# A depth-wise convolution of 31 taps: six tiles on TensorE with two positions per product, a shifted tile read by two transfers

## The chip, the cores and the metric

One core of a Trainium2 chip runs the whole program. The time is the device time of one execution in microseconds (us). Five engines each work through their own list of instructions: TensorE (PE), VectorE (DVE), ScalarE (ACT), GpSimd (POOL) and SyncE (SP). SP computes nothing and issues most of the transfers; POOL and ACT can issue transfers too. The transfers are carried by 16 DMA engines.

## What is computed

The program is one step of a network of four layers over 384 positions (128 of a prompt, 256 of a sample, each a sequence of its own) and 1024 channels. Each layer is a mixer and an MLP. The mixer of layer 1, the only one of its kind, is a convolution block:

```python
def _dwconv_centred(x, w, b):
    k = w.shape[0]
    lo = (k - 1) // 2
    hi = k - 1 - lo
    y = lax.conv_general_dilated(x, w[:, None, :], window_strides=(1,), padding=[(lo, hi)],
                                 dimension_numbers=('NWC', 'WIO', 'NWC'),
                                 feature_group_count=x.shape[-1])
    return y + b

def _conformer_conv(h, w_pw1, b_pw1, dw_w, dw_b, ln_g, ln_b, w_pw2, b_pw2):
    val, gate = jnp.split(h @ w_pw1 + b_pw1, 2, axis=-1)
    z = val * jax.nn.sigmoid(gate)
    z = _dwconv_centred(z, dw_w, dw_b)
    z = jax.nn.silu(_layernorm(z, ln_g, ln_b))
    return z @ w_pw2 + b_pw2
```

Here `w_pw1` is 1024 x 2048 and `dw_w` holds 31 taps for each of the 1024 channels. Everything is fp32.

## The kernel before

Channels lie on partitions, so a tensor of 1024 channels is eight tiles of 128 partitions by 384 positions. A dense fp32 product is split in high and low parts and done as three products (`mm3`). Weights come in chunks of 1 MB (`raw`, two buffers) and are split on ACT (`whi`) and DVE (`wlo`). PE runs through products of this kind while the transfers, ACT and DVE prepare the next chunk. Each engine takes its instructions in the order in which the build has put them: that of the code, moved in places by `issue_after`, which keeps what is written under it behind a named instruction.

The function `conformer` does the mixer of layer 1. For each tile m, `pwin(m)` runs the pw1 chunk on PE, and `glu` makes the gated tile on ACT (`gth`, `gv`) and DVE and writes it into `zp`, with zeros between and beside the two sequences. The convolution is then done in one of two ways. Tiles 0 and 1 are done on DVE, a multiply and add over 399 positions for each tap (`conv_dve`, L903). Tiles 2 to 7 are done on PE: `glu` writes `zp` to DRAM (`zd`, L854) and reads it back by four transfers, each into 32 partitions and shifted by one position more than the last (`z`, L857). A partition of `z` then holds four channels at one of four shifts, and one product with diagonals of taps (`dg`, L861, read from `diag`) sums four taps of 32 channels. A tile takes 8 steps of 4 groups of 32 channels: 32 products of 399 columns (`conv_mm`). The sums (`cps`, in PSUM) go directly to `zc`, on ACT for the tiles in FIRST (L885), else on DVE (L887). The buffer `z4` exists three times. The transfers for tiles 2 to 5 are issued by POOL, those for tiles 6 and 7 by SP.

The layer norm sums over channels, so over all eight tiles. A provisional mean from four tiles (FIRST; `shift`, products `mu1p`) is taken off first; `moments` then adds each tile into one sum (`me1a`) and its square into another (`va1a`). Tile 7 comes last and in two pieces (`stats`): the sample's 256 columns, then the prompt's 128. PE sums over channels by products with ones (`lnm` for the mean, `lnv` for the variance), and a short chain on ACT and DVE makes the factor of the norm. `normed` scales each tile, applies silu, and splits it (`yh`, `yl`) for the pw2 product (`p`). Weights of the modulation that are needed here (`pmwl`) are loaded by `lnload`, the last two into buffers of `z4`. `preload` brings an activation table to ACT ahead of its use.

Of the kernel before, what the change touches and what calls it, by code (L numbers as in the profile page):

```python
# [28 lines left out]
CG = SEQ + 15 + LAT  # L29
CSEG = ((0, 0, SEQ), (1, SEQ + 15, CG))  # L30
CP = CG + CW
PE_CONV = (2, 3, 4, 5, 6, 7)
TAP = CW // 4 + 1
SYNCZ = (6, 7)
CONVCUT = 20
ZW = CG + 4 * (TAP - 1)

# [55 lines left out]
FIRST = (2, 3, 0, 4)  # L93
# [26 lines left out]
def trunk(ctx, tc, wst, wmod, vecs, condr, xin, kcT, vcache, rpbt, diag, ident_in,  # L120
# [81 lines left out]
    loaded = {}  # L202

    def load_chunk(i):
# [616 lines left out]
    def conformer(l, j, nrm):  # L821
        mv = need(l, G1)
        with (tc.tile_pool(name=f"cf{l}", bufs=1) as cp,
              tc.tile_pool(name=f"cd{l}", bufs=1, space=bass.MemoryType.DRAM) as dp):
            zps = [cp.tile([P, CP], F32, tag="zp", name=f"zp{l}{i}", bufs=KT) for i in range(KT)]
# [4 lines left out]
            def glu(m, pv, pg, c=None):  # L830
# [14 lines left out]
                for s, a, b in SEG:  # L845
                    o = 15 + 15 * s
                    i = nc.vector.scalar_tensor_tensor(z[:, a + o:b + o], th[:, a:b], 1.0, v[:, a:b],
                                                       op0=ALU.add, op1=ALU.mult)
                glus.append(i.ins)
                if m in PE_CONV:  # L850
                    z4 = cp.tile([P, 4, ZW], F32, tag="z4", name=f"z4{l}{m}", bufs=3)
                    zd = dp.tile([P, CP], F32, tag="zd", name=f"zd{l}{m}", bufs=3)
                    dma = (nc.sync if m in SYNCZ else nc.gpsimd).dma_start
                    dma(zd, z)  # L854
                    zg = zd.rearrange("(g c) n -> c g n", g=4)
                    for s in range(4):
                        i = dma(z4[32 * s:32 * s + 32], zg[:, :, s:s + ZW])  # L857
# [21 lines left out]
            def conv_pe(m):  # L879
                zcs[m] = zc = cp.tile([P, N], F32, name=f"zc{l}{m}")  # L880
                ps = conv_mm(m, f"cps{l}{m}", 0, CG)
                for s, a, e in CSEG:
                    _, xa, xb = SEG[s]
                    if m in first:
                        nc.scalar.activation(zc[:, xa:xb], ps[:, a:e], AF.Identity, bias=dwb[:, m:m + 1])  # L885
                    else:
                        nc.vector.scalar_tensor_tensor(zc[:, xa:xb], ps[:, a:e], dwb[:, m:m + 1], mu[:, xa:xb],  # L887
# [502 lines left out]
```

## Time and profile before

| | us |
|---|---|
| median of 3 runs | 1750.3 (1749.62 to 1750.89) |
| profiled execution | 1750.85 |
| its span | 1748.7 |
| second pw1 piece of the chain to the last variance sum of the sample, within the span | 461.17 to 559.45 |

The granted TensorE clock over the span was 0.997 of full speed. The part that the change touches is some 100 us of 1749. In the profile a line like `x cps L131` names the engine's operation by the tile that it writes; L131 is the helper through which all products go, so products are told apart by tile names. For a transfer the profile gives the time of its issue on the queue of an engine (SPq is that of SP) and, apart from that, the time from issue to landing. Of the convolution's reads back from DRAM POOL issues 16 and SP 8, of 213.5 KB each.

### The profile page before, as it was taken

To read this page: it belongs to the slowest core of one execution; us is meant where nothing else is said; L and a number is where in the kernel's file an instruction comes from. 1 tells how busy PE (TensorE), PEld (TensorE's weight loads), DVE (VectorE), ACT (ScalarE), POOL (GpSimd) and SP (SyncE) were. 2 spreads that over 40 slices of the span, in tenths; PEclk is the share of its full clock that TensorE was granted. 3 is DMA by queue.
4 is the path that set the end of the run, shared out by engine and by line. 5 is a ranking of instruction groups with operands and counts; after the bars stand their busy time and mean duration, and the time that the engine had idled before them with its cause. 6 is when DMAs were issued, how large, how long until landed. Compare 5 with 4: busy or idle time off the path is not lost.

```text
span 1748.7 us, 27296 instructions
## 1 busy us (share of the span) xinstructions
PE 1723.2 (99%) x10442; PEld 1625.2 (93%) x10442; DVE 1404.8 (80%) x2791; ACT 945.0 (54%) x1697; POOL 16.1 (1%) x36
## 2 busy tenths in 40 slices
PE   8999999999999999999999999999999999999997
PEld 7779999999986999999987889999999789999997
DVE  5998999899897898889875668889999978843443
ACT  4876672454633774254465657524546976733531
POOL 0000000000020000000000000000000000000000
PEclk9999999999999999999999999999999999999999
DMA  9665367766486247767554433676774413533331
GB/s 389 236 219 177 128 225 254 239 246 236 159 237 180 97 139 259 240 219 241 195 182 140 133 99 130 205 240 235 242 241 162 155 49 121 174 128 121 124 135 43
DMA packets 67795, 322.42 MB, mean 184 GB/s; under 512 B 7952, under 2 KB 13456, under 8 KB 44496
## 3 DMA queue, kind: packets, MB, share of 16 engines
q1 hardware_dynamic: 66384, 316.30, 52.8%
q0 software_dynamic: 1280, 4.38, 1.0%
q8 instruction: 82, 1.34, 0.3%
q14 instruction: 49, 0.40, 0.1%
HBM read 316.69 MB, written 3.96 MB: 183 GB/s over the span
## 4 chain that ended last, share of the span: by engine, by line
PE 77%; DVE 15%; ACT 3%; issue 2%; DMA 2%; SPq 0%; DVEq 0%; ACTq 0%
PE f L131 29%; PE o L131 27%; PE pw L131 4%; PE lo L131 3%; DVE mjunk L331 3%; PE qk L131 3%; DVE wlo L219 2%; PE p L131 2%; PE wo L131 2%; PE cps L131 2%; PE v L131 2%; DVE xf L608 1%; DMA pmw<-wmod 1%; PE s L131 1%; PE po L131 1%
## 5 line engine op out<-in xcount | busy, mean ns | idle before, releaser
L218 ACT ACTIVATE whi<-raw 128x1024 fp32r<-128x1024 f32 x360 | 378.5, 1059 | 545.3 <-PE o L131 327.2
L219 DVE TENSOR_TENSOR wlo<-raw,whi 128x1024 fp32r<-128x1024 f32 x360 | 437.7, 1221 | 165.6 <-ACT whi L218 165.3
L331 DVE SCALAR_TENSOR_TENSOR mjunk<-dmw,condb 128x1024 bf16<-128x1024 f32 x308 | 375.3, 1219 | 1.5
L131 PE MATMUL o<-hl,whi 128*128 128x384 f32 x1024 | 343.0, 335 | 0.0
L131 PE MATMUL o<-hh,wlo 128*128 128x384 f32 x1024 | 343.0, 335 | 0.0
L131 PE MATMUL o<-hh,whi 128*128 128x384 f32 x1024 | 343.0, 335 | 0.0
L131 PEld LDWEIGHTS o<-hh,wlo 128*128 128x128 f32 x1024 | 192.2, 188 | 0.0
L131 PEld LDWEIGHTS o<-hh,whi 128*128 128x128 f32 x1024 | 192.2, 188 | 0.0
L131 PEld LDWEIGHTS o<-hl,whi 128*128 128x128 f32 x1024 | 192.2, 188 | 0.0
L501 DVE SCALAR_TENSOR_TENSOR x<-o,modv,x 128x128 f32<-128x128 f32 (+1 forms) x128 | 47.4, 412 | 69.0 <-PE o L131 69.0
L131 PE MATMUL g<-xf,graw 128*128 128x386 f32 x256 | 85.7, 490 | 1.7 <-DVE gl L666 1.7
L131 PEld LDWEIGHTS g<-xf,graw 128*128 128x128 f32 x256 | 47.9, 190 | 34.3 <-DVE gl L666 2.3
L785 DVE TENSOR_TENSOR hl<-s,hh 128x384 fp32r<-128x384 f32 x128 | 71.1, 555 | 6.6 <-ACT s L784 2.4
L783 ACT ACTIVATE hh<-r 128x384 fp32r<-128x384 f32 x128 | 67.1, 524 | 3.3
L784 ACT ACTIVATE s<-r 128x384 f32<-128x384 f32 x128 | 65.2, 509 | 0.0
L779 ACT ACTIVATE r<-f 128x384 f32<-128x384 f32 x112 | 53.0, 473 | 13.4 <-PE f L131 13.4
L131 PE MATMUL lo<-yh,wlo 128*128 128x384 f32 x128 | 43.5, 340 | 1.6 <-DVE wlo L219 1.6
L131 PE MATMUL lo<-yl,whi 128*128 128x384 f32 x128 | 43.0, 336 | 0.0
L131 PE MATMUL lo<-yh,whi 128*128 128x384 f32 x128 | 42.6, 336 | 0.0
L903 DVE SCALAR_TENSOR_TENSOR zt<-zp,vec,zt 128x399 f32<-128x399 f32 x58 | 36.7, 633 | 1.4
L131 PE MATMUL wo<-oT,whi 128*128 128x384 f32 x128 | 33.7, 343 | 0.0
L131 PE MATMUL cps<-z,dg 128*32 128x399 f32 (+2 forms) x448 | 32.8, 449 | 0.0
(1515 smaller groups left out, 4002.2 us busy)
## 6 DMA issues: line engine op xcount, KB each, us to landing
raw<-wst SPq DMA_DIRECT2D x180, 1024.0 KB, 5.0
dmw<-wmod SPq DMA_DIRECT2D x154, 512.0 KB, 4.1
pmw<-wmod SPq DMA_DIRECT2D x34, 512.0 KB, 6.8
graw<-wst SPq DMA_DIRECT2D x16, 512.0 KB, 4.8
bt<-rpbt SPq DMA_DIRECT2D x16, 384.0 KB, 3.5
z<-zd POOLq DMA_DIRECT2D x16, 213.5 KB, 6.7
dg<-diag SPq DMA_DIRECT2D x6, 512.0 KB, 4.1
pmwl<-wmod SPq DMA_DIRECT2D x4, 512.0 KB, 5.0
```

Of the source, the lines that this page charges most:

```text
L131: i = nc.tensor.matmul(*a, **kw)
L218: nc.scalar.activation(hi, raw[:, s], AF.Copy)
L219: nc.vector.tensor_tensor(lo, raw[:, s], hi.bitcast(F32), op=ALU.subtract)
L331: nc.vector.scalar_tensor_tensor(mjunk, w, 0.5, condb[:, s], op0=ALU.mult, op1=ALU.mult, accum_out=mod_tile(l)[:, c, m, s:s + 1]))
L501: nc.vector.scalar_tensor_tensor(x[m][:, xa:xb], ps[:, a:b], mv[:, g, m, s:s + 1], x[m][:, xa:xb], op0=ALU.mult, op1=ALU.add)
L608: nc.vector.scalar_tensor_tensor(xf, r[:, k:k + LG], lcw[:, j, t, k:k + 1], xf, op0=ALU.mult, op1=ALU.add)
L779: nc.scalar.activation(r, ps[:, :N], AF.Relu)
L783: nc.scalar.activation(hh, r, AF.Square)
L784: nc.scalar.activation(s, r, AF.Square)
L785: nc.vector.tensor_tensor(hl, s, hh.bitcast(F32), op=ALU.subtract)
L903: nc.vector.scalar_tensor_tensor(t, z[:, k:k + CG], dww[:, m, k:k + 1], t, op0=ALU.mult, op1=ALU.add)
```

## The change

Tiles 1 to 6 are done on PE with two positions in one product; tile 7 stays with one position per product, and only tile 0 is left on DVE. For tiles 1 to 6 `glu` writes the even and the odd positions of `zp` apart, and the copy in DRAM is kept so. The shifted tile is read by two transfers of 64 partitions, one for each parity. Each has four shifts outermost, then 16 rows of channels, then one run of 1717 numbers that spans eight channels' rows. A partition thus holds eight channels at one of eight shifts. A product has 32 output rows, 16 channels by two neighbouring positions, and 200 columns: 2 halves of the channels, 4 steps, 4 groups, so 32 products of 200 columns for a tile (`conv_pair`). The rows of its result alternate between the two positions. ACT copies it from PSUM (`co`), and four transfers on ACT's queue bring it to `zq`, where a partition holds one channel. `conv_in` adds the bias and takes off the mean, on ACT for tiles 1 to 3, on DVE for tiles 4 to 6.

Tile 7's shifted tile is read by one transfer to 128 partitions, with four shifts outermost, 32 rows, and a run of 1724. The channels of tiles 1 to 7 then have another order on the partitions behind the convolution; the rows of pw2, the bias and the factors of the norm are put in that order on the host. The provisional mean comes from tiles 0 to 3, and its products move ahead of the end of the last pw1 chunk. The transfers of tile 5 move from POOL's queue to SP's. The third `pmwl` gets a buffer of its own and the other three use those of `z4`. `preload` moves ahead of the copy of tile 6, and the first part of pw2 is kept behind the norm's instructions of tile 5. Left out below are declarations of names, values handed back for `issue_after`, and the lists of inputs.

```diff
-CG = SEQ + 15 + LAT
-CSEG = ((0, 0, SEQ), (1, SEQ + 15, CG))
-CP = CG + CW
-PE_CONV = (2, 3, 4, 5, 6, 7)
+CGAP = 16
+CG = SEQ + CGAP + LAT
+CSEG = ((0, 0, SEQ), (1, SEQ + CGAP, CG))
+CP = CG + CW + 1
+PAIR_CONV = (1, 2, 3, 4, 5, 6)
+LAST = 7
 TAP = CW // 4 + 1
-SYNCZ = (6, 7)
-CONVCUT = 20
+SYNCZ = (5, 6, 7)
 ZW = CG + 4 * (TAP - 1)
+CU = CG // 2
+PV = CU + 15
+PZ = CU + 12
+ZB = 2 * (PV + 1) + 8
+ZT = 3 * CP + ZW
+PT = 7 * PV + PZ
...
-FIRST = (2, 3, 0, 4)
+FIRST = (0, 1, 2, 3)
...
-            nc.scalar.activation(hi, raw[:, s], AF.Copy)
-            nc.vector.tensor_tensor(lo, raw[:, s], hi.bitcast(F32), op=ALU.subtract)
+            a = nc.scalar.activation(hi, raw[:, s], AF.Copy)
+            b = nc.vector.tensor_tensor(lo, raw[:, s], hi.bitcast(F32), op=ALU.subtract)
+            copied[i] = a.ins, b.ins
...
-                    o = 15 + 15 * s
-                    i = nc.vector.scalar_tensor_tensor(z[:, a + o:b + o], th[:, a:b], 1.0, v[:, a:b],
-                                                       op0=ALU.add, op1=ALU.mult)
+                    o = 15 + CGAP * s
+                    dst, p, q = z[:, a + o:b + o], th[:, a:b], v[:, a:b]
+                    if m in PAIR_CONV:
+                        o = a // 2 + 8 * s
+                        dst = z[:, 7:7 + 2 * PV + 2].rearrange("p (f v) -> p f v", f=2)[:, :, o:o + (b - a) // 2]
+                        p, q = (t.rearrange("p (v f) -> p f v", f=2) for t in (p, q))
+                    i = nc.vector.scalar_tensor_tensor(dst, p, 1.0, q, op0=ALU.add, op1=ALU.mult)
                 glus.append(i.ins)
-                if m in PE_CONV:
-                    z4 = cp.tile([P, 4, ZW], F32, tag="z4", name=f"z4{l}{m}", bufs=3)
-                    zd = dp.tile([P, CP], F32, tag="zd", name=f"zd{l}{m}", bufs=3)
-                    dma = (nc.sync if m in SYNCZ else nc.gpsimd).dma_start
-                    dma(zd, z)
-                    zg = zd.rearrange("(g c) n -> c g n", g=4)
-                    for s in range(4):
-                        i = dma(z4[32 * s:32 * s + 32], zg[:, :, s:s + ZW])
+                dma = (nc.sync if m in SYNCZ else nc.gpsimd).dma_start
+                if m == LAST or m in PAIR_CONV:
+                    z4 = cp.tile([P, ZT], F32, tag="z4", name=f"z4{l}{m}", bufs=3)
+                    dg = wp.tile([P, D], F32, tag="dmw", name=f"dg{l}{m}", bufs=3)
+                    if m == LAST:
+                        zd = dp.tile([P, CP], F32, name=f"zd{l}{m}")
+                        dma(zd, z[:, :CP])
+                        i = dma(z4, bass.AP(zd.tensor, zd.offset, [[1, 4], [4 * CP, 32], [1, ZT]]))
+                        z4 = [z4[:, g * CP:g * CP + ZW] for g in range(4)]
+                        dg = dg.rearrange("p (t n) -> p t n", t=TAP)
+                        nc.sync.dma_start(dg, diag)
+                    else:
+                        zd = dp.tile([2, P, PV], F32, tag="zd", name=f"zd{l}{m}", bufs=3)
+                        dma(zd.rearrange("f p v -> p f v"), z[:, :2 * PV].rearrange("p (f v) -> p f v", f=2))
+                        for t in range(2):
+                            i = dma(z4[64 * t:64 * t + 64, :PT],
+                                    bass.AP(zd.tensor, zd.offset + (1 - t) * P * PV, [[1, 4], [8 * PV, 16], [1, PT]]))
+                        z4 = [z4[:, g * PV:g * PV + PZ] for g in range(8)]
+                        dg = dg.rearrange("p (k g n) -> p k g n", k=4, g=8)
+                        nc.sync.dma_start(dg, pairw[PAIR_CONV.index(m)])
                     zds.append(i.ins)
-                    z4s[m] = z4
-                    dgs[m] = wp.tile([P, D], F32, tag="dmw", name=f"dg{l}{m}", bufs=3).rearrange("p (t n) -> p t n", t=TAP)
-                    nc.sync.dma_start(dgs[m], diag[PE_CONV.index(m)])
-
-            z4s, dgs, convs = {}, {}, []
+                    z4s[m], dgs[m] = z4, dg
+
+            z4s, dgs, zqs, evs, convs = {}, {}, {}, {}, []
...
-                                             z4s[m][:, g, 4 * t + a:4 * t + b], start=t == 0, stop=t == TAP - 1)
+                                             z4s[m][g][:, 4 * t + a:4 * t + b], start=t == 0, stop=t == TAP - 1)
...
+            def pairs(t, xa, xb):
+                return t[:, xa:xb].rearrange("p (v f) -> p f v", f=2)
+
+            def conv_pair(m):
+                ps = mm_tile(f"cps{l}{m}")[:, :CG].rearrange("p (r u) -> p r u", r=2)
+                for r in range(2):
+                    for k in range(4):
+                        for g in range(4):
+                            i = matmul(ps[32 * g:32 * g + 32, r], dgs[m][:, k, 2 * g + r],
+                                       z4s[m][2 * g + r][:, 4 * k:4 * k + CU], start=k == 0, stop=k == 3)
+                convs.append(i.ins)
+                o = cp.tile([P, 2, CU], F32, tag="co", name=f"co{l}{m}", bufs=2)
+                zq = cp.tile([P, 2, CU], F32, tag="zq", name=f"zq{l}{m}", bufs=2)
+                nc.scalar.activation(o, ps, AF.Copy)
+                for r in range(2):
+                    for f in range(2):
+                        evs[m] = nc.scalar.dma_start(zq[r:P:2, f], o[f:P:2, r]).ins
+                zqs[m] = zq
+
+            def conv_in(m):
                 zcs[m] = zc = cp.tile([P, N], F32, name=f"zc{l}{m}")
-                ps = conv_mm(m, f"cps{l}{m}", 0, CG)
                 for s, a, e in CSEG:
                     _, xa, xb = SEG[s]
+                    src = zqs[m][:, :, a // 2:e // 2]
                     if m in first:
-                        nc.scalar.activation(zc[:, xa:xb], ps[:, a:e], AF.Identity, bias=dwb[:, m:m + 1])
+                        nc.scalar.activation(pairs(zc, xa, xb), src, AF.Identity, bias=dwb[:, m:m + 1])
                     else:
-                        nc.vector.scalar_tensor_tensor(zc[:, xa:xb], ps[:, a:e], dwb[:, m:m + 1], mu[:, xa:xb],
+                        nc.vector.scalar_tensor_tensor(pairs(zc, xa, xb), src, dwb[:, m:m + 1], pairs(mu, xa, xb),
                                                        op0=ALU.add, op1=ALU.subtract)
...
-                    if i > 3:
-                        t = cp.tile([P, 4, ZW], F32, tag="z4", name=f"pmwl{i}", bufs=3)
-                        t = t.rearrange("p a b -> p (a b)")[:, :D]
+                    if i > 2:
+                        t = cp.tile([P, ZT], F32, tag="z4", name=f"pmwl{i}", bufs=3)[:, :D]
                     elif i > 1:
-                        t = cp.tile([P, D], F32, tag="pm", name=f"pmwl{i}", bufs=2)
+                        t = cp.tile([P, D], F32, name=f"pmwl{i}")
...
             conv_dve(0)
             pwin(3)
             pwin(4)
+            conv_pair(1)
+            conv_pair(2)
+            with tc.issue_after(evs[2]):
+                conv_in(1)
             pwin(5)
-            conv_pe(2)
-            conv_pe(3)
-            lnload(0, 4)
+            conv_pair(3)
+            with tc.issue_after(gvs[-1]):
+                conv_in(2)
+            lnload(0, 3)
             ensure(state["w"] + 3)
             pwin(6)
-            conv_dve(1, 0, CONVCUT)
+            with tc.issue_after(gvs[-1]):
+                conv_in(3)
             ensure(state["w"] + 3)
+            last, (hi, lo) = state["pe"], copied[state["w"]]
+            with tc.issue_after(last), tc.issue_after(hi), tc.issue_after(lo):
+                shift()
             pwin(7)
-            with tc.issue_after(glus[-1]), tc.issue_after(gvs[-1]), tc.issue_after(zds[-1]):
-                conv_dve(1, CONVCUT, CW)
-            conv_pe(4)
-            shift()
-            conv_pe(5)
-            center(1)
-            conv_pe(6)
+            conv_pair(4)
+            conv_pair(5)
+            with tc.issue_after(evs[5]):
+                conv_in(4)
+            preload(AF.Abs_reciprocal_sqrt, zcs[4][:, 0:1])
+            conv_pair(6)
+            with tc.issue_after(evs[6]):
+                conv_in(5)
+                conv_in(6)
             for m in range(KT):
                 for s, a, b in SEG:
                     nc.scalar.activation(x[m][:, a:b], x[m][:, a:b], AF.Identity, bias=gb[:, m, s:s + 1])
-            preload(AF.Abs_reciprocal_sqrt, zcs[6][:, 0:1])
-            lnload(4, LNPRE)
+            lnload(3, LNPRE)
...
-            return out_proj(l, "pw2", j, y, f"p2{l}")
+            with tc.issue_after(zds[-1]), tc.issue_after(ths[5]), tc.issue_after(tvs[5]):
+                return out_proj(l, "pw2", j, y, f"p2{l}")
...
+    turn = np.arange(D).reshape(KT, P)
+    for m in PAIR_CONV:
+        turn[m] = turn[m].reshape(16, 4, 2).transpose(1, 0, 2).reshape(P)
+    turn[LAST] = turn[LAST].reshape(32, 4).T.reshape(P)
+    turn = turn.reshape(D)
...
-            c = _mm(i["conf_w_pw2"][j], (2 * b, 2 * b + 1))
+            c = _mm(i["conf_w_pw2"][j][turn], (2 * b, 2 * b + 1))
...
-    diag = np.zeros((len(PE_CONV), P, TAP, P), f4)
     w = i["conf_dw_w"][0]
+    diag = np.zeros((P, TAP, P), f4)
     ch = np.arange(32)
-    for n, m in enumerate(PE_CONV):
-        for t in range(TAP):
-            for s in range(4):
-                if 4 * t + s < CW:
-                    for g in range(4):
-                        diag[n, 32 * s + ch, t, 32 * g + ch] = w[4 * t + s, m * P + 32 * g + ch]
+    for t in range(TAP):
+        for s in range(4):
+            if 4 * t + s < CW:
+                for g in range(4):
+                    diag[32 * s + ch, t, 32 * g + ch] = w[4 * t + s, LAST * P + 4 * ch + g]
+    pairw = np.zeros((len(PAIR_CONV), P, 4, 8, 32), f4)
+    ch = np.arange(16)
+    for n, m in enumerate(PAIR_CONV):
+        for k in range(4):
+            for t in range(8):
+                for f in range(2):
+                    if 0 <= 8 * k + t - f < CW:
+                        for g in range(8):
+                            pairw[n, t % 2 * 64 + t // 2 * 16 + ch, k, g, 2 * ch + f] = w[8 * k + t - f, m * P + 8 * ch + g]
```

SP's order around the last pw1 chunks, before: the write of a tile (`zd`), its four reads (`z`), first for tile 6, then for tile 7, between weights (`raw`, `pmwl`) and diagonals (`dg`).

```order
L212 DMA raw_5932<-wst 128x2048
L854 DMA zd_5395<-zp_4651 128x430
L857 DMA z_5394<-zd_5395 32x4x427 x4
L854 DMA zd_5492<-zp_4652 128x430
L861 DMA dg_5498<-diag 128x1024
L212 DMA raw_6094<-wst 128x2048
L857 DMA z_5491<-zd_5492 32x4x427 x4
L167 DMA pmwl_5675<-wmod 128x1024
```

After, the same stretch holds tiles 5, 6 and 7.

```order
L220 DMA raw_5455<-wst 128x2048
L876 DMA zd_5315<-zp_4650 128x2x215
L882 DMA dg_5446<-pairw 128x1024
L878 DMA z_5313<-zd_5315 64x1x1717 x2
L876 DMA zd_5447<-zp_4651 128x2x215
L878 DMA z_5445<-zd_5447 64x1x1717 x2
L869 DMA zd_5548<-zp_4652 128x432
L873 DMA dg_5547<-diag 128x1024
L870 DMA z_5546<-zd_5548 128x1x1724
L174 DMA pmwl_5710<-wmod 128x1024
L220 DMA raw_5969<-wst 128x2048
L174 DMA pmwl_5712<-wmod 128x1024
```

Tile 5's transfers are now in this queue, its read stands ahead of tile 6's write, and a `pmwl` and a `raw` follow tile 7's read at once.

PE from the end of the last pw1 chunk on, before: `cps` are the convolutions of tiles 4, 5, 6 and 7.

```order
L131 MATMUL cps_5513<-z_5154,dg_5161 32x399 x32
L131 MATMUL mu1p<-zc_5238,ones 128x384
L131 MATMUL mu1p<-zc_5274,ones 128x384
L131 MATMUL mu1p<-zc_4979,ones 128x384
L131 MATMUL mu1p<-zc_5512,ones 128x384
L131 MATMUL cps_5574<-z_5229,dg_5236 32x399 x32
L131 MATMUL cps_5619<-z_5394,dg_5401 32x399 x32
L131 MATMUL cps_5684<-z_5491,dg_5498 32x256 x32
L131 MATMUL lnm_5720<-me1a,ones 128x256
```

After:

```order
L138 MATMUL cps_5552<-z_5157,dg_5158 32x200 x32
L138 MATMUL cps_5592<-z_5313,dg_5314 32x200 x32
L138 MATMUL cps_5640<-z_5445,dg_5446 32x200 x32
L138 MATMUL cps_5721<-z_5546,dg_5547 32x256 x32
L138 MATMUL lnm_5757<-me1a,ones 128x256
L138 MATMUL lnm_5757<-zc_5720,ones 128x256
```

The mean's four products have left this place, the three tiles 4 to 6 have 200 columns, and both `lnm` products now stand together ahead of `lnv`.

ACT from the gate of tile 7 on, before: `zc` takes tile 4 out of PSUM, `va1q` is the first of seven squares, after six of which the table load stands.

```order
L834 ACTIVATE gth_5485<-pw_1_5460,hb_219 128x384
L835 ACTIVATE gv_5486<-pw_0_5435,hb_219 128x384
L885 ACTIVATE zc_5512<-cps_5513,vec 128x128
L885 ACTIVATE zc_5512<-cps_5513,vec 128x256
L930 ACTIVATE mu_4661<-mu1p 128x384
L359 ACTIVATE va1q_5554<-zc_5238 128x384
```

After, from the same gate:

```order
L843 ACTIVATE gth_5540<-pw_1_5515,hb_219 128x384
L844 ACTIVATE gv_5541<-pw_0_5490,hb_219 128x384
L915 ACTIVATE co_5585<-cps_5552 128x400
L918 DMA zq_5586<-co_5585 64x200 x4
L915 ACTIVATE co_5625<-cps_5592 128x400
L918 DMA zq_5626<-co_5625 64x200 x4
L368 ACTIVATE va1q_5636<-zc_5632 128x384
L353 ACT_TABLE_LOAD
L353 ACTIVATE one<-zc_5632 128x1
L915 ACTIVATE co_5673<-cps_5640 128x400
L918 DMA zq_5674<-co_5673 64x200 x4
L368 ACTIVATE va1q_5684<-zc_5680 128x384
```

The direct evacuation of tile 4 is replaced by a copy and four transfers for each of tiles 4, 5 and 6, and the table load stands between the copies of tiles 5 and 6.

More of the change, by code (lines that the diff above doesn't have):

```diff
@@ L119, in trunk @@
 @with_exitstack
-def trunk(ctx, tc, wst, wmod, vecs, condr, xin, kcT, vcache, rpbt, diag, ident_in,
+def trunk(ctx, tc, wst, wmod, vecs, condr, xin, kcT, vcache, rpbt, diag, pairw, ident_in,
           y_out, st_out, k_out, v_out):
@@ L202, in trunk @@
     loaded = {}
+    copied = {}
     def load_chunk(i):
@@ L338, in newton @@
         nc.vector.scalar_tensor_tensor(b, b, -0.5 / n, r, op0=ALU.mult, op1=ALU.mult)
-        nc.vector.scalar_tensor_tensor(r, b, 1.5, r, op0=ALU.add, op1=ALU.mult)
+        return nc.vector.scalar_tensor_tensor(r, b, 1.5, r, op0=ALU.add, op1=ALU.mult).ins
     one = cst.tile([P, 1], F32, name="one")
@@ L824, in conformer @@
               tc.tile_pool(name=f"cd{l}", bufs=1, space=bass.MemoryType.DRAM) as dp):
-            zps = [cp.tile([P, CP], F32, tag="zp", name=f"zp{l}{i}", bufs=KT) for i in range(KT)]
+            zps = [cp.tile([P, ZB], F32, tag="zp", name=f"zp{l}{i}", bufs=KT) for i in range(KT)]
             for z in zps:
@@ L874, in conv_mm @@
                         i = matmul(ps[32 * g:32 * g + 32, :], dgs[m][:, t, 32 * g:32 * g + 32],
-                                             z4s[m][:, g, 4 * t + a:4 * t + b], start=t == 0, stop=t == TAP - 1)
+                                             z4s[m][g][:, 4 * t + a:4 * t + b], start=t == 0, stop=t == TAP - 1)
                 convs.append(i.ins)
                 return ps
-            def conv_pe(m):
+            def pairs(t, xa, xb):
[16 more added lines that the diff above has]
+            def conv_in(m):
                 zcs[m] = zc = cp.tile([P, N], F32, name=f"zc{l}{m}")
-                ps = conv_mm(m, f"cps{l}{m}", 0, CG)
                 for s, a, e in CSEG:
                     _, xa, xb = SEG[s]
+                    src = zqs[m][:, :, a // 2:e // 2]
                     if m in first:
-                        nc.scalar.activation(zc[:, xa:xb], ps[:, a:e], AF.Identity, bias=dwb[:, m:m + 1])
+                        nc.scalar.activation(pairs(zc, xa, xb), src, AF.Identity, bias=dwb[:, m:m + 1])
                     else:
-                        nc.vector.scalar_tensor_tensor(zc[:, xa:xb], ps[:, a:e], dwb[:, m:m + 1], mu[:, xa:xb],
+                        nc.vector.scalar_tensor_tensor(pairs(zc, xa, xb), src, dwb[:, m:m + 1], pairs(mu, xa, xb),
                                                        op0=ALU.add, op1=ALU.subtract)
@@ L1017, in normed @@
                 th = tmp(f"lth{l}{m}{a}")[:, :e - a]
-                nc.scalar.activation(th, zc, AF.Tanh, scale=hg[:, m:m + 1], bias=hb[:, m:m + 1])
+                ths[m] = nc.scalar.activation(th, zc, AF.Tanh, scale=hg[:, m:m + 1], bias=hb[:, m:m + 1]).ins
                 za = tmp(f"lza{l}{m}{a}")[:, :e - a]
@@ L1023, in normed @@
                     nc.vector.tensor_scalar(za, zc, lng[:, m:m + 1], lnb[:, m:m + 1], op0=ALU.mult, op1=ALU.add)
-                nc.vector.scalar_tensor_tensor(th, th, 1.0, za, op0=ALU.add, op1=ALU.mult)
+                tvs[m] = nc.vector.scalar_tensor_tensor(th, th, 1.0, za, op0=ALU.add, op1=ALU.mult).ins
                 split(th, hi[:, a:e], lo[:, a:e])
@@ L1028, in conformer @@
             rs = stats(0)
+            ths, tvs = {}, {}
             held = []
@@ L1034, in conformer @@
                 if m % 4 == 0:
-                    y4 = cp.tile([P, 4, ZW], F32R, tag="z4", name=f"yl{l}{m}", bufs=3)
-                    y4 = y4.rearrange("p a b -> p (a b)")
+                    y4 = cp.tile([P, ZT], F32R, tag="z4", name=f"yl{l}{m}", bufs=3)
                 hi = cp.tile([P, CP], F32R, tag="zp", name=f"yh{l}{m}", bufs=KT)
@@ L1327, in lay_out @@
                            cols(i["lru_lambda"]), cols(i["state_lru"][0]),
-                           cols(i["conf_b_pw1"][0].reshape(2, D)), dww, cols(i["conf_dw_b"][0]),
-                           cols(i["conf_ln_g"][0]), cols(i["conf_ln_b"][0]), cols(i["conf_b_pw2"][0]),
+                           cols(i["conf_b_pw1"][0].reshape(2, D)), dww, cols(i["conf_dw_b"][0][turn]),
+                           cols(i["conf_ln_g"][0][turn]), cols(i["conf_ln_b"][0][turn]), cols(i["conf_b_pw2"][0]),
                            cols(i["final_g"])], axis=1)
@@ L1358, in lay_out @@
     return dict(wst=wst, wmod=wmod, vecs=vecs, condr=condr, xin=xt, kcT=kcT, vcache=vc, rpbt=rpbt,
-                diag=diag, ident_in=ident)
+                diag=diag, pairw=pairw, ident_in=ident)
 _OUTS = [("y_out", (KT, P, N)), ("st_out", (2, P, 2, KT)), ("k_out", (KT, P, SEQ)), ("v_out", (SEQ, D))]
@@ L1364 @@
         ("xin", (KT, P, N)), ("kcT", (KT, P, SEQ)), ("vcache", (SEQ, D)), ("rpbt", (KT, P, 2, 2, N)),
-        ("diag", (len(PE_CONV), P, TAP, P)), ("ident_in", (P, P))]
+        ("diag", (P, TAP, P)), ("pairw", (len(PAIR_CONV), P, 4, 8, 32)), ("ident_in", (P, P))]
 def build(nc):
```

## The prediction

> **What bounds the kernel now.** I read the page's line of busy time first, then the chain of waits through the convolution, then what PE waits for.
>
> ```profile
> PE 1723.2 (99%) x10442; PEld 1625.2 (93%) x10442; DVE 1404.8 (80%) x2791; ACT 945.0 (54%) x1697; POOL 16.1 (1%) x36
> ...
> 507.18 10.87 PE cps L131 x109
> 518.05 16.87 PE pw L131 x96
> 534.91 5.50 PE cps L131 x61
> 540.41 2.78 PE mu1p L131 x8
> 543.19 14.32 PE cps L131 x173
> 557.51 0.63 PE lnm L131 x2
> ...
> 559.00 0.45 PE lnv L131 x2
> ```
>
> PE is busy 99% of the span, and the chain through the stage is PE alone from the last pw1 products to the variance sums (lnv): 507.18 to 559.45. So a product that goes from here is worth its full time, as long as the next one has its data. The only PE wait listed between 455 and 640 us is the first output product:
>
> ```profile
> PE p L131 <- ACT yh L407: 2.7, 1, 2.7
> ...
> 568.00:570.00 2.00, 1.20 (x4) 1.20 (x5) 2.00 (x7) 2.00 (x5) 0.00 (x0) 0.66 0.00 0
> 570.00:572.00 2.00, 2.00 (x9) 2.00 (x8) 1.74 (x5) 1.97 (x5) 0.00 (x0) 0.50 0.00 0
> 568.80 2.93 PE p L131 x8
> 576.12 23.91 PE p L131 x136
> ```
>
> The first row is the wait; the next two are windows of 2 us (the last three figures are granted clock, DMA share and GB/s), the last two pieces of the chain. After a PE pause of 2.7 us the granted clock is 0.66, then 0.50. Eight products then take 2.93 us where 136 take 23.91 (0.176 each, so 1.41). A pause of some microseconds therefore costs about **1.5 us** more than itself. This tail behind lnv has the same steps after the change, so I measure the gain or loss at lnv.
>
> **The change, part by part.** PE: a tile of 399 columns takes 10.87/2 = 5.45 us. Two smaller pieces bound one of 200 columns:
>
> ```profile
> 559.36 1.96 PE L131 MATMUL cps<-z,dg 128*32 128x128 f32 x64
> 561.25 0.49 PE L131 MATMUL lnm<-me1a,ones 128*128 128x128 f32 x2
> ```
>
> 128 columns take 561.25 - 559.36 = 1.9 us, and 256 take what the last piece of cps (14.32) has beside two whole tiles: 3.4. By interpolation 200 columns take 2.75 (5.45 x 200/399 = 2.73 is the lower end, 3.4 the upper); I take 2.8. Five tiles go (27.25), six come (16.8): **10.45 us less PE**, 2.85 of which the new tile 1 has given back.
>
> DVE: one tile's taps go.
>
> ```profile
> L903 DVE SCALAR_TENSOR_TENSOR zt<-zp,vec,zt 128x399 f32<-128x399 f32 x58 | 36.7, 633 | 1.4
> ...
> 554.90 0.56 DVE L372 TENSOR_TENSOR me1a<-me1a,zc 128x384 f32<-128x384 f32 x1
> ```
>
> About 29 x 0.63 = 18 us of DVE, hidden behind PE already: worth nothing itself. The strided reads and writes (even and odd positions) aren't in the trace; per operation I bound them by 0 and by 0.4 (one more small operation), and take 0, since DVE has the 18 us to give before the last tile.
>
> Up to the end of the last pw1 chunk PE barely moves. A chunk lasts 16.87/2 = 8.43, so chunk 5 began, and chunk 4 ended, at 507.18 - 8.43 = 498.75. From there, after the change: cps1 and cps2 (5.6) to 504.4, chunk 5 to 512.8, cps3 to 515.6, chunk 6 to 524.0, the mean (mu1p, 2.78, moved ahead of chunk 7 and into its start) to 526.8, chunk 7 to **535.2** (534.91 before). From there cps4, 5 and 6 take 8.4 instead of mu1p and three of 5.45: tile 7's product could start at 543.6, where before it started at 543.19 + 10.9 = 554.1. So 10.5 us can be had if tile 7's shifted copy is there. That is where I see the end set.
>
> ```profile
> 530.46 0.33 SPq L854 DMA_DIRECT2D zd<-zp  x1
> 533.88 2.11 SPq L857 DMA_DIRECT2D z<-zd  x4
> 537.69 0.34 SPq L854 DMA_DIRECT2D zd<-zp  x1
> ```
>
> From the end of a chunk to the write to DRAM (zd): 537.69 - 534.91 = 2.8 (the gate on ACT and DVE, then the issue, the same three steps as before). From that to the first read back (z): 533.88 - 530.46 = 3.4. Now the read itself:
>
> ```profile
> q1 hardware_dynamic: 66384, 316.30, 52.8%
> ...
> z<-zd SPq DMA_DIRECT2D x8, 213.5 KB, 5.4
> ...
> DMA to landing us min/median/max: 3.2/6.6/8.5
> ...
> raw<-wst SPq DMA_DIRECT2D x180, 1024.0 KB, 5.0
> ...
> 556.00:558.00 2.00, 2.00 (x31) 1.17 (x24) 0.43 (x2) 0.00 (x0) 0.00 (x0) 1.00 0.98 389
> ```
>
> While its packets are in flight the queue moves 316.30 MB/(0.528 x 16 x 1748.7 us) = 21.4 KB/us for one of the 16 engines, in the best window 389/16/0.98 = 24.8; I take 23. Before, each of four reads walks 32 rows outermost. Now the source pattern has the shift outermost, a count of 4, then 16 or 32 rows, then one long run of 6.9 KB. **I forecast that a transfer is shared out by that outermost count**, so four engines carry it and twelve stand idle. None of the reads of before in this stage has an outermost count under 32, so their rows can't show it: the two ends are a sixteenth per engine (a raw of 1024 KB lands in 5.0) and a quarter. I take the quarter, since each read that is seen to fill 16 engines has a multiple of 16 outermost and 4 is none, and keep the other as rival A.
>
> [...]
>
> A shifted tile is 128 x 6868 bytes = 879 KB, 220 KB for each of four engines: 9.6 us at 23, plus a fixed part of 3.2 (the quickest z) less its own share on 16 engines (213.5/16/23 = 0.6), 2.6. Together **12.2 us**. In order on SP:
> - z5: written at 512.8 + 2.8 = 515.6, read from 519.0, lands 531.2.
> - zd6 is issued at 526.8 behind it and lands near 532; z6 from there, lands 544.2. So cps6, ready at 535.2 + 5.6 = 540.8, waits 3.4 us and ends at 547.0.
> - zd7 is issued at 538.0, lands at 544.8 behind z6; z7 lands at **557.0**, 2.9 us later than tile 7's product started before.
> - PE has then stood 10 us: 3.4 + 1.5 for 256 columns, to 561.9.
>
> The new evacuation runs beside that: PSUM to co on ACT, four transfers on ACT's queue into zq, then zc. The four transfers are issued in order on ACT, and by the built order those of tile 6 are held until z7 has landed and, the last, until the first pmwl behind it has: 512 KB on 16 engines at 23 are 1.4 us.
>
> ```profile
> k_out<-kc SPq DMA_DIRECT2D x8, 64.0 KB, 1.8
> ...
> 554.13 0.74 DVE L887 SCALAR_TENSOR_TENSOR zc<-cps,vec,mu 128x128 f32<-128x128 f32 x2 [1.24 <-PE cps L131]
> ```
>
> So the last is issued at 557.0 + 1.4 + 0.5 = 558.9 (an issue takes 2.11/4, about 0.5), and 50 KB land in about 2.3 (64 KB in 1.8, with some traffic): 561.2. Then zc6 and its sum (0.74 + 0.56) to 562.5, when lnm starts (557.51 before). **Sum: +5.0 us.** The profiled execution took 1750.85 (span 1748.7), 0.55 over the median 1750.3, so 1755.85 on its basis and **1755.3** on the median's. With 24.8 KB/us three reads save 2.1 (+2.9: 1753.2), with 21.4 they cost 2.1 more (+7.1: 1757.4).
>
> The other edits: normalisation, table load and held-back copies of pw2 keep their order on PE. The table load (1.28 us on ACT) now stands between tile 5's and tile 6's co, beside the wait for z6; without that cover it is 1.3 us at most. The copies of the third pw2 chunk may cost the tail 0 to 1 us; I take 0, since DVE and ACT idle while z7 is awaited. pmwl 5 waits for tile 7's last product and is wanted after it, as before.
>
> **The rivals.**
>
> A, sixteen engines carry the reads. For it: before, z and raw fill them (0.98 and 389 GB/s in one window). Then z7 is read from 541.2 (538.0 + 3.2) and lands 5.0 later, as a raw does, at 546.2. Product 256 with the low clock ends at 551; zq6's last transfer is issued at 548.5 and, with pmwl and raw beside it, lands near 551.3; zc6 and its sum go to 552.6, against 557.51: -4.9, and the pause costs up to 1.5 again: -3.4, **1746.9**. Not all of the 10.5, since tile 7's chain of transfers takes over. The point from which it decides: three reads in a row carry the +5.0, so at 12.2 - 5.0/3 = 10.5 us a read the change breaks even, and below that it is faster.
>
> C, as A, but zq is slow among other transfers:
>
> ```profile
> 487.53 2.19 POOL L857 DMA_DIRECT2D z<-zd  x4 [2.05 <-DMA zd<-zp]
> ...
> 501.44 2.18 POOL L857 DMA_DIRECT2D z<-zd  x4 [7.14 <-DMA zd<-zp]
> ```
>
> In the second row a small write took 7.1 us where weights were read at the same time. With pmwl and raw issued right beside zq6, 548.5 + 7.1 + 1.3 = 556.9: -0.6, with a slow clock behind it +0.4: **1750.7**. Against it: ACT's queue holds only zq.
>
> D, the opposite end of the stage: four engines, and POOL's reads of tiles 1 and 2 are late as well. They are issued near 487, where the first row has the first read of before, and wanted at 498.7 and 501.4; at 12.2 each one after the other the second lands at 511, so PE would wait for cps2. It decides if POOL's reads share one set of four. A wait there of some 6 us is partly lost in that of tile 7 (z5 to z7 follow pw5, which comes later too): +5 on top, **1760.5**. This is the worse of the two slower cases; four engines alone is already slower.
>
> That the products don't halve is excluded by the 128 and 256 columns above.
>
> **How the numbers follow.** Four engines 0.47, A 0.32, C 0.12, D 0.09. A measurement here can tell about 0.2%, 3.5 us: faster is below 1746.8, slower above 1753.8. Of four engines 0.40 lies above 1753.8 and 0.07 (quick engines) within; A's 1746.9 lies on the edge, 0.18 faster and 0.14 within; C 0.02, 0.08 and 0.02; D is slower. Together faster 0.20, same 0.29, slower 0.51. The likeliest case's own range is 1753.2 to 1757.4. The whole range takes in C, D's 1760.5 and A down to 1746.5: 1746.5 to 1761, with some 0.15 left below and 0.04 above.
>
> **What would show it.** Right: z5, z6 and z7 land about 12 us after issue with the DMA share near a quarter; PE waits for z ahead of cps6 and of tile 7's product; cps of 200 columns at 2.8. Wrong: z lands in 4 to 6 us with all engines filled (A), then the wait ahead of lnm is on zq. If the first wait of PE is ahead of cps2, it is D. It would also be wrong if PE's pause ahead of tile 7 left the clock at full, which takes 1.5 off each slower case.

## The result, and the profile after

| | before | after |
|---|---|---|
| median, us | 1750.6 (1749.62 to 1752.51, 4 runs) | 1808.44 (1804.91 to 1809.8, 4 runs) |
| ratio | | 1.0324, 95% interval 1.0311 to 1.0337 |
| profiled execution, us | 1750.85 | 1808.54 |
| its span, us, and granted clock | 1748.7, 0.997 | 1806.8, 0.979 |

The change costs 57.8 us where the sum of the forecast had 5.0. The page of the changed kernel, its line of busy time and two lines of transfers (count, KB each, median us to landing):

```profile
PE 1726.1 (96%) x10506; PEld 1634.8 (90%) x10506; DVE 1386.6 (77%) x2760; ACT 946.7 (52%) x1703; POOL 13.1 (1%) x28
...
z<-zd POOLq DMA_DIRECT2D x8, 429.2 KB, 16.3
...
pmwl<-wmod SPq DMA_DIRECT2D x4, 512.0 KB, 22.1
```

PE lost three points of its share, and half a shifted tile takes 16.3 us to land where a quarter took 6.7. One window shows the whole stage, from the first pw1 product to the first output product: length, then busy time of PE, PEld, DVE, ACT and POOL, then clock, DMA share and GB/s. Before:

```profile
456.58:568.80 112.22, 109.36 (x955) 87.55 (x953) 97.41 (x200) 54.90 (x108) 14.35 (x28) 1.00 0.63 190
```

After:

```profile
458.79:626.95 168.16, 111.70 (x1019) 96.75 (x1018) 78.08 (x167) 56.41 (x112) 11.32 (x20) 0.82 0.58 144
```

The stage is 55.9 us longer. PE is idle 56.5 us in it (168.16 - 111.70) against 2.9, and busy 2.3 longer although its work is shorter: the clock averages 0.82. (The first experiment's kernel has the same products; PE is busy 102.6 us with them, at a clock of 0.97.) PE's waits in the stage (us in total, times, longest):

```profile
PE cps L138 <- DMA z<-zd: 32.7, 2, 17.7
PE cps L138 <- issue: 11.9, 1, 11.9
PE mu1p L138 <- ACT zc L927: 5.4, 1, 5.4
PE lnm L138 <- DVE me1a L381: 4.2, 1, 4.2
PE p L138 <- ACT yh L416: 2.2, 1, 2.2
```

The second row is a wait for a shifted tile too: the view of the reads (`z`) puts 44.6 us in three waits of PE down to them, which is the first two rows together. The chain that ended last names what those waits stand on (start, us, what):

```profile
489.12 18.71 DMA z<-zd
507.83 5.13 issue
512.96 4.70 PE cps L138 x62
...
520.06 11.18 DMA zq<-co
...
534.39 11.05 DMA raw<-wst
...
548.47 13.55 DMA zd<-zp
...
563.38 17.19 DMA zd<-zp
...
580.64 22.33 DMA z<-zd
...
605.14 6.92 DMA zq<-co
...
613.67 2.04 PE lnm L138 x4
```

Before, this stretch of the chain was PE alone. Now it is one transfer after another: a read of tile 1 (18.7 us; its other half is the one behind the issue row), an evacuation, a weight chunk, the writes of tiles 6 and 7 to DRAM (13.6 and 17.2 us for 215 KB), the read of tile 7 (22.3). SP's writes of this size landed in 3.2 us before the change. Here the first of the two lands at 562.02, just as the read ahead of it ends (DMA share 0.24 from 558 to 560 us, 0.08 from 560 to 562), and a window in which tile 5's read is nearly alone shows what a read occupies:

```profile
548.00:562.00 14.00, 13.71 (x106) 12.30 (x110) 7.12 (x15) 4.72 (x9) 0.00 (x0) 0.78 0.25 77
```

DMA share 0.25, 77 GB/s: four of sixteen engines, at 77/4 = 19 KB/us each, for both halves of the tile together. In the records of the packets exactly four are in flight for 93% of the time from 550 to 558 us.

### The profile page after: what moved, and what is told of

Read it like the earlier page. It is cut to its first block, busy times and chain, and to the rows that moved or that the text cites. A ratio compares the mean times of both kernels' runs of the same rounds, so it can differ in the third digit from the quotient of the medians.

```text
span 1806.8 us, 27423 instructions
## 1 busy us (share of the span) xinstructions
PE 1726.1 (96%) x10506; PEld 1634.8 (90%) x10506; DVE 1386.6 (77%) x2760; ACT 946.7 (52%) x1703; POOL 13.1 (1%) x28
## 4 chain that ended last, share of the span: by engine, by line
PE 71%; DVE 15%; DMA 7%; ACT 4%; issue 2%; ACTq 0%; SPq 0%; DVEq 0%
PE f L138 28%; PE o L138 26%; PE lo L138 3%; DVE mjunk L340 3%; PE qk L138 3%; DVE wlo L227 2%; DMA z<-zd 2%; PE wo L138 2%; PE p L138 2%; DMA zd<-zp 2%; PE v L138 1%; DVE xf L617 1%; DMA zq<-co 1%; DMA raw<-wst 1%; PE pw L138 1%
## 5 line engine op out<-in xcount | busy, mean ns | idle before, releaser
L138 PE MATMUL cps<-z,dg 128*32 128x200 f32 (+2 forms) x512 | 30.3, 406 | 44.6 <-DMA z<-zd 32.7
L138 PEld LDWEIGHTS cps<-z,dg 128*32 128x32 f32 x512 | 19.7, 134 | 55.1 <-DMA z<-zd 18.1
## 6 DMA issues: line engine op xcount, KB each, us to landing
z<-zd POOLq DMA_DIRECT2D x8, 429.2 KB, 16.3
pmwl<-wmod SPq DMA_DIRECT2D x4, 512.0 KB, 22.1
```

The source lines that it names most:

```text
L138: i = nc.tensor.matmul(*a, **kw)
```

## The experiments

All times are medians; those of one run are beside kernels before of 1751 to 1752.

### Rows outermost in every read

```diff
-  bass.AP(zd.tensor, zd.offset, [[1, 4], [4 * CP, 32], [1, ZT]])
+  bass.AP(zd.tensor, zd.offset, [[4 * CP, 32], [1, 4], [1, ZT]])
-  ..., [[1, 4], [8 * PV, 16], [1, PT]]
+  ..., [[8 * PV, 16], [1, 4], [1, PT]]
...
-  diag[32 * s + ch, t, ...
+  diag[s + 4 * ch, t, ...
...
-  pairw[n, t % 2 * 64 + t // 2 * 16 + ch, ...
+  pairw[n, t % 2 * 64 + t // 2 + 4 * ch, ...
```

> The reads of tiles 1 to 7 walk the rows outermost (16 or 32) and the four shifts inside; the taps' rows are put in that order on the host. Nothing else changes. Theory (a count of 4 outermost puts a read on four DMA engines, and what is queued behind it on these four waits too): a shifted tile lands in 4 to 8 us instead of 13 to 22, PE waits for no shifted tile longer than 2 us, and the time is 1743 to 1752. Rival 1 (the loss sits in the new evacuation, four transfers on ACT's queue for each tile): zq still takes about 10 us, time over 1775. Rival 2 (long runs of 6.9 KB that overlap in DRAM are slow on any number of engines): a tile still takes over 12 us, time over 1780.

1752.39 (10 runs), ratio to the kernel before 1.0007, interval 0.9997 to 1.0017. The bytes, the transfers and the order of every engine are those of the change; only the order of the two outer dimensions differs, and 56 of the 57.8 us are gone. Its transfers of 520 to 560 us, SP's reads (median us to landing):

```profile
z<-zd SPq DMA_DIRECT2D x4, 429.2 KB, 5.0
...
z<-zd SPq DMA_DIRECT2D x1, 862.0 KB, 4.7
```

And a window in which tile 6's read runs nearly alone:

```profile
536.00:538.00 2.00, 2.00 (x16) 1.75 (x18) 0.92 (x2) 0.00 (x0) 0.00 (x0) 1.00 0.97 244
```

The share is 0.97 with 244 GB/s, and tile 7 lands in 4.7 us instead of 22. Rival 1 (the evacuation) and rival 2 (long runs) both fall as causes of the loss. Two details of the expectation missed: PE waits 2.5 us, not under 2, for a shifted tile, and the median is 0.4 above the expected 1743 to 1752. What the experiment shows as the cause is the order of the two dimensions; whether it acts by the number of engines alone is the question of the next ones.

### Which reads cost how much

The same edit for tile 7 alone, for tiles 1 to 6 alone, and for tiles 1 to 4 alone (`FOUR` lists the tiles that keep the change's pattern):

```diff
+FOUR = (5, 6, 7)
-  ..., [[1, 4], [8 * PV, 16], [1, PT]]
+  ..., [[1, 4], [8 * PV, 16], [1, PT]] if m in FOUR else [[8 * PV, 16], [1, 4], [1, PT]]
```

> Only tile 7's read walks the rows outermost; tiles 1 to 6 keep the four shifts outermost. Theory: tile 7 lands in 5 to 8 us instead of 22, and tile 6's evacuation, held behind it, comes some 15 us sooner; the waits of tiles 1 to 6 stay: 1788 to 1796. Rivals 1 and 2: within 5 of 1808.

> Only tiles 1 to 6 read the rows outermost; tile 7 keeps the four shifts outermost. Theory: no wait for tiles 1 to 6; tile 7 alone on four engines lands 14 to 18 us after its issue near 541, so about 557, and the time is 1752 to 1760, what the prediction gave for one such read in place of three in a row. Rival 1: over 1775.

> Tiles 5, 6 and 7, the reads that SP issues, keep the change's pattern (four shifts outermost); tiles 1 to 4 walk the rows outermost. This is the case that the prediction priced at +5 us over the kernel before. If its queue arithmetic holds and only the rate per engine was too high (12 to 18 KB/us measured against 23 assumed), z5 lands near 533, z6 near 550, z7 near 571, tile 7's product starts some 17 us later than before: 1768 to 1780. If the rest of the loss was all on POOL's reads: 1753 to 1758.

Measured: 1791.89 (tile 7 mended), 1768.18 (tiles 1 to 6 mended), 1788.54 (tiles 1 to 4 mended). The first is as expected. The two parts add up: 1808.4 - 1791.9 = 16.5 and 1808.4 - 1768.2 = 40.3, together 56.8 against 56.0 for both. So tile 7's read alone costs 16 us and the three reads of SP 1788.5 - 1752.4 = 36. Mending POOL's four gives back 1808.4 - 1788.5 = 20; no kernel has these four alone on the change's pattern.

The last two are 8 us over the ends of what was expected, and both show why. SP's queue with tiles 5 to 7 on four engines:

```profile
526.42 1.24 SPq L879 DMA_DIRECT2D z<-zd  x2
528.89 0.38 SPq L877 DMA_DIRECT2D zd<-zp  x1
543.19 1.11 SPq L879 DMA_DIRECT2D z<-zd  x2
544.40 0.39 SPq L870 DMA_DIRECT2D zd<-zp  x1
...
559.33 0.54 SPq L871 DMA_DIRECT2D z<-zd  x1
```

And from the last read on in that kernel's chain:

```profile
559.33 24.82 DMA z<-zd
...
586.31 6.60 DMA zq<-co
...
594.52 2.05 PE lnm L139 x4
```

Each tile's write is issued behind the read of the tile before, and the next read 14 to 15 us later: a period of 16.8 and 16.1 us where the forecast had 13.0 and 12.8 (reads at 519.0, 532 and 544.8). Tile 7's read takes 24.8, with weights beside it, and 20.5 in the kernel in which it alone is on four engines (14 to 18 was expected). That kernel shows what weights and such a read do to each other:

```profile
550.00:552.00 2.00, 0.00 (x0) 0.00 (x0) 0.00 (x0) 0.00 (x0) 0.00 (x0) 0.50 1.07 226
...
560.00:562.00 2.00, 0.00 (x0) 0.00 (x0) 0.00 (x0) 0.00 (x0) 0.00 (x0) 0.50 0.24 68
```

In the second row the read is alone: 0.24, 68 GB/s. In the first, weights are moving too and all engines count as busy, but they move 226 GB/s where 389 were seen at a share of 0.98 before the change.

### POOL's queue instead of SP's

```diff
-SYNCZ = (5, 6, 7)
+SYNCZ = (7,)
```

> All reads but tile 7's are issued by POOL; the patterns are those of the change. If a read of POOL goes to any four engines in turn and one of SP always to the same four, the two halves of tiles 5 and 6 run side by side and land in 7 to 11 us instead of 13 to 16, and DMA share while they run alone is 0.5 in place of 0.25: 1790 to 1803. If POOL uses the same four engines as SP: within 4 of 1808.

1805.84 in one run: the time is that of the second case. The window in which tile 5's two halves are alone says the first:

```profile
556.00:558.00 2.00, 2.00 (x14) 2.00 (x13) 1.97 (x5) 0.53 (x1) 0.00 (x0) 1.00 0.51 120
```

Two halves on POOL's queue keep eight engines busy (0.51), where two halves on SP's keep four (0.25). But eight engines move 120 GB/s, 15 KB/us each against 19, and POOL's later reads still wait for their writes (18.0, 12.3 and 8.6 us for those of tiles 3, 4 and 6). The time alone would have told the wrong story.

In the change, then, POOL's reads hardly left engines idle. Two windows over the reads of tiles 1 and 2 with weights beside them, of the change and of the kernel with rows outermost everywhere:

```profile
490.00:500.00 10.00, 10.00 (x59) 10.00 (x59) 5.92 (x10) 1.05 (x2) 2.34 (x4) 1.00 1.00 182
```

```profile
490.00:500.00 10.00, 10.00 (x68) 9.67 (x70) 7.01 (x12) 3.06 (x4) 0.95 (x2) 1.00 1.03 303
```

All engines are busy in both, but with the shifts outermost they move 182 GB/s and with the rows outermost 303, 11 KB/us for an engine against 18. So in these runs the order does two things: it sets the number of engines (shares of 0.25 and 0.97 for reads of SP alone), and with the shifts outermost each engine also moves less (11 against 18). By these rows the lateness of tiles 1 and 2 comes from the second; how SP's 36 us divide between the two was not measured.

### A count of four with rows of its own, a count of eight

Based on the first experiment; tile 7 in eight transfers of four rows, and all tiles in transfers of eight rows:

```diff
+for j in range(8):
+    i = dma(z4[16 * j:16 * j + 16], bass.AP(zd.tensor, zd.offset + 16 * j * CP, [[4 * CP, 4], [1, 4], [1, ZT]]))
...
+for j in range(4):
+    i = dma(z4[32 * j:32 * j + 32], bass.AP(zd.tensor, zd.offset + 32 * j * CP, [[4 * CP, 8], [1, 4], [1, ZT]]))
...
+for t in range(4):
+    i = dma(z4[32 * t:32 * t + 32, :PT],
+            bass.AP(zd.tensor, zd.offset + (1 - t // 2) * P * PV + t % 2 * 64 * PV, [[8 * PV, 8], [1, 4], [1, PT]]))
```

> As e1, but tile 7 is read by eight transfers of four rows, rows outermost: again a count of 4, so four engines, but each engine walks rows of its own instead of four engines walking the same rows. If the low rate comes from four engines on the same rows of DRAM: some 21 KB/us for each engine, so the tile lands in 10 to 13 us and the time is 1757 to 1762. If a read on four engines is as slow with any rows: 17 to 21 us and 1765 to 1770, like e3. If the transfers are not held to four engines: within 3 of e1.

> As e1 (rows outermost, all seven tiles), but each transfer holds eight rows, so the count outermost is 8: four transfers for a tile in place of two or one. Theory: eight engines carry the reads, the same eight on SP; DMA share is near 0.5 while they run alone, a tile lands in 8 to 10 us, and the time lies between e1 and the change, nearer e1: 1754 to 1768. Rival (the count only matters where it is 4, or what counts is that four engines walked the same rows): within 3 of e1.

1760.31 and 1755.69, one run each. Both times lie in the range of the first theory, but they settle little. Tile 7 of the first kernel lands 17.5 us after its first issue (543.17 to 560.66), which is what the second theory had. The second kernel's time lies within the runs of the kernel with rows outermost everywhere (1749.67 to 1756.95). The windows say more. With such reads running, of the first kernel and of the second:

```profile
548.00:550.00 2.00, 0.00 (x0) 0.00 (x0) 0.00 (x0) 1.14 (x3) 0.00 (x0) 0.50 0.16 60
```

```profile
526.00:528.00 2.00, 2.00 (x12) 1.87 (x12) 0.00 (x0) 0.41 (x1) 0.00 (x0) 1.00 0.51 185
```

With 8 outermost the share is 0.51, with 16 it was 0.97, with 4 it was 0.25: in these three the number of engines follows the count. At the same share of 0.51 POOL's reads with the shifts outermost moved 120 GB/s, these 185.

Eight transfers for tile 7 bring no more engines: still at most four, at 60/(0.16 x 16) = 23 KB/us each. That is more than the 17.7 (68/(0.24 x 16)) of four engines on the same rows, and neither window has weights in it. The tile is late all the same: SP takes 9.4 us to issue the eight, and the last, issued at 551.96, has weights beside it from 553.66 on. Why engines that walk the same rows move less is left open.

### What keeps the repaired version from being faster

With rows outermost PE is busy 102.6 us in the stage (457.15 to 571.57) against 109.4 before, 6.8 less, and the time is the same as before. PE's waits in that kernel:

```profile
PE lnm L138 <- DVE me1a L381: 5.5, 1, 5.5
PE cps L138 <- DMA z<-zd: 2.5, 1, 2.5
PE p L138 <- ACT yh L416: 2.3, 1, 2.3
PE cps L138 <- issue: 1.3, 1, 1.3
```

And the last part of its chain:

```profile
545.22 6.50 DMA zq<-co
551.74 0.47 ACTq L918
...
552.53 3.70 DMA zq<-co
...
557.91 2.05 PE lnm L138 x4
```

Here is in kind the end that the prediction described: the sums wait for tile 6's evacuation, whose last transfers are held until one of tile 5's has landed (6.50 us). Two edits follow. Tile 6 is done like tile 7, without an evacuation by transfers; and a small transfer out of tile 5's `zq` keeps SP from issuing later weights until that has landed:

```diff
-PAIR_CONV = (1, 2, 3, 4, 5, 6)
-LAST = 7
+PAIR_CONV = (1, 2, 3, 4, 5)
+ONE_CONV = (6, 7)
...
+            conv_one(6)
...
+            gate = cp.tile([2, 2, 1], F32, name=f"gate{l}")
+            gate = nc.sync.dma_start(gate, zqs[5][0:2, :, 0:1]).ins
...
+            with tc.issue_after(gate):
+                lnload(3, LNPRE)
```

`conv_one` is `conv_mm` over 400 columns with DVE taking the sums. The first of these kernels has no gate; the fourth has six paired tiles and the gate; the third leaves the first `pmwl` ahead of the gate.

> As e1, with tile 6 done like tile 7: one position per product, sums taken from PSUM by DVE without the four transfers. PE pays 2.65 us. Theory: what e1 gives back at the end is the wait for tile 6's evacuation (5.5 us ahead of lnm, and the low clock behind it); the longer product covers the read of tile 7, and lnm follows tile 7's product without a wait: 4 to 6 us below e1, 1745.5 to 1748.5. Rival: tile 7's read is late anyway and DVE's sums come last: within 1.5 of e1.

> As v1, with a transfer of 16 bytes out of tile 5's zq put on SP's queue behind tile 7's read: SP can issue the later pmwl and raw only when tile 5's evacuation has landed. Theory: the evacuation is late because some 4 MB of weights are issued beside it (9.5 us from issue to landing in v1, DMA share 1.0); with the gate it lands 2.5 to 4 us after its last issue, lnm starts near 553 instead of 558.5 without a wait over 1.5 us, and the time is 1744 to 1748. Rival: short rows of 800 bytes or the order on ACT's queue make it slow whatever runs beside it: zq as late as in v1, and the time as v1 or 1 to 3 us more, since the weights come later.

> As v3, but the first pmwl stays ahead of the gate; the later pmwl and the raw chunks stay behind it. In v3 PE waited 2.4 us for pmwl ahead of the modulation's products (pmp) at the end. Theory: that wait goes, the evacuation of tile 5 comes at most 1 us later: 1746 to 1748.5. Rival: half a MB more beside the evacuation costs as much as it saves: within 0.7 of v3.

> As e1 (six tiles with two positions, rows outermost) with the same gate behind tile 6's evacuation. Theory: the last zq lands some 2 us sooner than in e1, lnm still waits for it 2 to 4 us: 1747.5 to 1750.5. Rival: within 1 of e1.

| kernel | median, us | ratio to before | interval |
|---|---|---|---|
| tile 6 direct | 1753.28 | 1.0013 | 1.0004 to 1.0022 |
| and the gate | 1748.68 | 0.9986 | 0.9977 to 0.9995 |
| first pmwl ahead of the gate | 1749.74 | 0.9992 | 0.9983 to 1.0001 |
| six paired tiles and the gate | 1751.58 | 1.0 | 0.9991 to 1.0009 |

The first missed: removing tile 6's evacuation only showed that tile 5's was just as late. The wait in its chain:

```profile
545.74 9.45 DMA zq<-co
```

And a window over that wait:

```profile
546.00:556.00 10.00, 5.76 (x92) 2.50 (x84) 1.97 (x6) 2.01 (x4) 0.00 (x0) 1.00 1.00 389
```

The last 50 KB wait 9.5 us while weights fill all engines. With the gate, in the chain:

```profile
545.86 5.70 DMA zq<-co
...
560.47 6.01 DMA pmwl<-wmod
```

And over the shorter wait:

```profile
546.00:551.50 5.50, 5.21 (x84) 2.47 (x80) 1.45 (x3) 2.02 (x3) 0.00 (x0) 1.00 0.64 220
```

The share falls to 0.64, the transfer takes 5.7 us (2.5 to 4 was expected), and a wait for `pmwl` appears at the end, since it now starts later. So the weights were a cause and not the only one. This kernel is 0.14% faster than the one before the change, the only one of the four whose interval lies below 1, and 60 us faster than the change. Moving `pmwl` back ahead of the gate took that wait away (2.4 to 0.5 us) and gave the evacuation 7.1 us; it is no better. With six paired tiles the gate gains nothing that the measurement can tell. Of the expectations for these three, the gate's missed by 0.7 us, the one for the first `pmwl` lies below the result in both its cases, and for the fourth kernel the rival held.

## Why the prediction was wrong

- **Four engines.** Right for SP's reads, and it was the step that carried most weight. Shares of 0.25, 0.51 and 0.97 for counts of 4, 8 and 16, and PE's two longest waits ahead of the products of tiles 6 and 7, as forecast. The sum has tiles 5, 6 and 7 read by the same four; that was the author's estimate, and no run shows it, since the reads came one after another (issued at 546.42, 562.16 and 580.64 in the changed kernel); the runs showed both halves of tile 5 on four engines together (0.25), and writes of 13.6 and 17.2 us between one read and the next. The quick engines that the chances allow for were not seen: the shifted reads ran at 15 to 23 KB/us for an engine without weights beside them.
- **"I take 23."** This term failed. 21.4 and 24.8 came from the whole queue and from a window of weights, which aren't this kind of transfer. The trace of before had a window in which the shifted reads ran nearly alone:

```profile
538.00:540.00 2.00, 2.00 (x32) 0.67 (x23) 1.89 (x4) 0.00 (x0) 0.00 (x0) 1.00 0.85 202
```

  202/(0.85 x 16) = 14.9 KB/us, so 220/14.9 + 2.6 = 17.4 us a read instead of 12.2, and three in a row some 16 us more. With four engines on the change's pattern and no weights the runs show 17.7 to 19 KB/us, 14 to 15 us a read by the same sum, and 24.8 us with weights beside the read, which no term held. The case priced at +5 measured +37.5 (1788.54 against 1751). At the start of `lnm` it is 32.0 late (594.52 against 562.5): 7.4 come from tile 5's read being issued at 526.4, not at 519.0, 7.1 from the periods (16.8 and 16.1 against 13.0 and 12.8), 12.6 from tile 7's read, and 4.9 from what follows it (10.4 us to `lnm` instead of 5.5, of which the last transfer to `zq` took 6.6 and not 2.3). The 7.4 aren't due to SP's reads: with rows outermost everywhere that read is issued at 526.80. There tile 5's gate stands on ACT behind a `zc`, and ACT idles 7.7 us until an evacuation has landed; the forecast took the gate as before.
- **POOL's reads costed at nothing but in case D.** This was the second step that failed. Mending tiles 1 to 4 gives back 20 us. D had 0.09 and one wait of 6 us (its +5 on 1755.3 is 1760.3, not 1760.5). It came nearest by luck: its condition, that POOL's reads share one set of four, isn't what the windows show (1.00 from 490 to 500 us, 0.51 for two halves alone), and the first wait was ahead of tile 1's product, not tile 2's. The engines were busy with these reads and with weights, at 11 KB/us each. Measured, the first paired product began at 512.96 instead of 498.75, in a stage that began 2.2 us later: already 12 us late.
- **What stands behind a slow read.** Writes behind reads were in the forecast, with tiles 6 and 7, landing less than 1 us after the read. Of the weights it held the first `pmwl` behind tile 7's read, with 1.4 us. Measured, a `raw` chunk is in the chain with 11 us, and a `pmwl` landed in 22.
- **The pause of the clock.** Its size, 1.5 us, was that of one pause of 2.7 us. With pauses of up to 17.7 us the clock stood at 0.50 in 24 of the 65 windows of 2 us from 484 to 614 us (0.82 on average in the stage), and PE was busy 111.7 us in it, where the same products take 102.6 with rows outermost.
- **PE's work.** Right: 200 columns take 2.89 us in the repaired kernel, forecast 2.8. PE's busy time in the stage fell by 6.8 us there, not by 10.45; its clock was 0.97 in the stage.
- **Rival A, 1746.9.** The repaired kernel gave 1752.39. Its read of tile 7 took 4.7 us as A had it (forecast 5.0), and PE waited 2.5 for it (2.6 by A's times, 546.2 - 543.6). But the last pw1 chunk ended at 537.97, not at 535.2, and the evacuation came late, as in C: `lnm` started at 557.91, where A had 552.6 and C (1750.7) 556.9.
- **The range** ended at 1761, since D was added on as a single wait. Where the parts were measured apart they add up (16.5 + 40.3 against 56.0); they don't overlap.

## What to carry to other kernels

Read a transfer's rate from a window in which that kind of transfer runs alone, and look at its outermost dimension before its bytes: four shifts there cost 56 us, through fewer engines (a share of 0.25 against 0.97) and less from each (11 KB/us against 18 with weights beside them), and exchanging two dimensions brought them back. When a transfer takes few engines, price everything that is queued behind it, weights and small writes too (here a `pmwl` landed in 22.1 us instead of 5.0, a write in 17.2 instead of 3.2), and every queue that issues such reads (half a tile on POOL's took 16.3 us). Before trusting a saving on the busiest engine, ask which transfer ends last once it is gone: here 6.8 us less of busy PE bought nothing until tile 6 lost its evacuation and weights were held back behind tile 5's, and then 2.5.

## What the runs showed that was not expected

A read on four engines and the weights beside it moved less together than the two rates seen alone add up to: 226 GB/s at a DMA share of 1.07, against 389 at 0.98 for weights before the change. Four engines at 17.7 and twelve at 24.8 KB/us, as each was seen alone, would by the author's estimate move some 368. And a DMA share near 1 isn't a rate: reads of shifted rows on sixteen engines move 244 GB/s at 0.97.
